# Score tiles in a third PSUM bank, and latent attention head by head, in a two-block transformer kernel

## The chip, the cores and the metric

The kernel runs on one core of a Trainium2 chip. The metric is device time in microseconds (us) from a run on the chip. Five engines work side by side, each through its own instructions in their order: TensorE (PE in the profile; its weight loads have a row of their own, PEld), VectorE (DVE), ScalarE (ACT), GpSimd (POOL) and SyncE (SP), which here only issues transfers. Matmuls write to PSUM, which has eight banks of 128 x 512 fp32 numbers; GpSimd doesn't reach PSUM.

## The reference

Everything is fp32, for 512 positions of width 1024. A first block (chunked attention, convolution, gated feed-forward) is followed by two layers with other attentions, each with a gated embedding behind it. The change touches the two later attentions:

```python
# windowed_gqa: 16 heads, 4 key heads, window of 128 around each position
logits = einsum('bqkgd,bskd->bkgqs', q_blk, k_blk) * scale - slopes * dist   # masked
probs = softmax(concatenate([logits, sink_col]))[..., :-1]
o = einsum('bkgqs,bskd->bqkgd', probs, v_blk)
return (o * silu(z)) @ w_out

# mla (latent attention): 16 heads, every position sees all 512 keys
q = (rms_norm(cq, q_norm) @ w_qb)          # 64 plain + 32 rotated columns a head
kv = (rms_norm(ckv, kv_norm) @ w_kvb)      # 64 key + 64 value columns a head
q_rope = rotate(q_rope, cos, sin)
logits = (q_nope . k_nope + q_rope . k_rope) * scale
o = softmax(logits) @ v
return (o * silu(z)) @ w_out
```

## The kernel before

Activations lie with channels on partitions, as [128, 512] tiles. A product in nearly full precision is made of three passes: each operand is split into a high and a low part (`act_hi`, `act_lo`, `w_hi`, `w_lo`), and `mm3` (L345 to L347) issues high x high, low x high and high x low into one bank. A projection tile (`tile`) is eight such triples, or two or three in latent attention, in a bank of the ring `mm`.

PSUM's eight banks are divided by `ps(tag)`: three `mm` for projections, two `s` for scores, two `pt` for turned probabilities and sums, one `o` for the attention's products.

`attention` (L598) is a generator shared by three attentions; a class `Spec` of each gives its parts. It works through pairs of heads. An item `t` is one tile of 128 queries of one head: (pair p, half hf of the queries, tile ii of the half, head hh of the pair). In order of time an item goes through

- `scores(t)`: `qk` into a bank `s` (L1406 in windowed attention, two matmuls; L1750 in latent attention, three), a row maximum on VectorE (L1419 or L1755), an exponential on ScalarE out of the bank into a tile `P`;
- `scale(t-1)`: reciprocal of the row sum (L617), and the multiplication by it, on GpSimd in both later attentions (L257);
- `turn(t-lag)`: up to four 128 x 128 transposes into a bank `pt` (L635), and a copy on ScalarE to a tile `PT`;
- `product(p, hf)` (L666): probabilities times values for both heads of the pair, each with weights of 64 columns, into the bank `o`, at raised priority. `spec.out` then multiplies by the gate (`tA` on VectorE), and splits the result into `o_hi` (ScalarE) and `o_lo` (VectorE) for the output projection.

Latent attention ran its items half by half: both heads of queries 0 to 255, their product, then both heads of queries 256 to 511 and their product. Windowed attention (`whole`) ran both halves' products together after the second.

`drive` interleaves the attention's generator with the projections (`main`) by a share, and the framework's scheduler then orders the instructions of each engine: by the order in which they were written (a raised priority goes first), by buffers that come free in their ring, and by its own reckoning of when operands are there. So the order on an engine has to be looked at in the built program.

In latent attention two pairs share a group of weights: a pair with an even number has a tile more, the rotated query columns of four heads (`evac_qr`). They go through a chain of several engines, `rotated`: copy from PSUM to `tA` (ScalarE), shuffle (VectorE, L1603), product with the sines (GpSimd, L1604), product with the cosines and sum (VectorE), `act_hi` (ScalarE), `act_lo` (VectorE), and then four transfers a pair into `Qm` (SP, L1700). Scores of the next pair need them. `put` fills the rest of `Qm` and `Km` from PSUM, with two ScalarE and two VectorE instructions each (ACT L260 `Qm<-ps_mm`, DVE L253).

Of the kernel before, what the change touches and what calls it, by code (L numbers as in the profile page):

```python
# [7 lines left out]
F32 = mybir.dt.float32  # L8
# [8 lines left out]
T = 512  # L17
# [213 lines left out]
class Kernel:  # L231
# [366 lines left out]
    def attention(self, spec, pairs, ready, s):  # L598

        nc = self.nc  # L600
        items = [(p, hf, ii, hh) for p in range(pairs) for hf in range(2) for ii in range(2) for hh in range(2)]
        n = len(items)
        P, L, PT, O = {}, {}, {}, {}

        def scores(t):
            p, hf, ii, hh = items[t]
            i = 2 * hf + ii
            ps = self.ps("s")
            spec.qk(ps, p, hh, i)
            sb = s.tile([128, spec.width], F32, tag="P", name="P", bufs=spec.lag + 1)  # L610
            st = s.tile([128, 2], F32, tag="st", name="st", bufs=8)
            P[t] = spec.softmax(ps, sb, st, p, hh, i)
            L[t] = st

        def scale(t):
            st = L.pop(t)
            nc.vector.reciprocal(out=st[:, 0:1], in_=st[:, 1:2])  # L617
            if spec.scale_act:
                self.act(P[t], P[t], AF.Copy, scale=st[:, 0:1])
            else:  # L620
                self.ts(P[t], P[t], st[:, 0:1], 1.0, MUL, MUL, eng=nc.gpsimd)

        def turn(t):
            p, hf, ii, hh = items[t]
            i = 2 * hf + ii
            js = spec.keys(i)
            if (p, hf) not in PT:
                if spec.packed:
                    PT[p, hf] = s.tile([128, 2, 5, 128], F32, tag="PT", name="PT", bufs=3)
                else:  # L630
                    PT[p, hf] = s.tile([128, 2, spec.nj, 256], F32, tag="PT", name="PT", bufs=3 if spec.whole else 2)
            ps = self.ps("pt")
            x = P.pop(t)
            for a, j in enumerate(js):
                nc.tensor.transpose(ps[:, 128 * a:128 * a + 128], x[:, 128 * a:128 * a + 128], self.ident)  # L635
            j0 = js[0] - spec.first(hf)
            if spec.packed:
                b = (2 + hf) * ii
                out = PT[p, hf][:, hh, b:b + len(js)]
            else:  # L640
                out = PT[p, hf][:, hh, j0:j0 + len(js), 128 * ii:128 * ii + 128]
            src = ps[:, :128 * len(js)].rearrange("p (a q) -> p a q", q=128)
            if spec.turn_act(t):
                self.act(out, src, AF.Copy)
            else:
                nc.vector.tensor_copy(out=out, in_=src)

        def turned(pt, hh, hf, j, c0, c1):

            a = j - spec.first(hf)  # L650
            if not spec.packed:
                return pt[:, hh, a, c0:c1]
            if c1 - c0 == 256:
                return pt[:, hh, a:a + 3:2]
            return pt[:, hh, 0 if hf else 4]

        def product(p, hf):
            if p not in O:
                O[p] = self.ps("o")
            pt = PT.pop((p, hf))  # L660
            js = spec.order(hf)

            with self.tc.high_priority():
                for n_, (j, c0, c1) in enumerate(js):
                    for hh in (1, 0):
                        nc.tensor.matmul(  # L666
                            out=O[p][64 * hh:64 * hh + 64, 256 * hf + c0:256 * hf + c1], lhsT=spec.v(p, hh, j),
                            rhs=turned(pt, hh, hf, j, c0, c1), start=(n_ == 0), stop=(n_ == len(js) - 1),
                            skip_group_check=True,
                        )  # L670
            if hf == (0 if spec.whole else 1):
                spec.out(p, O.pop(p))

        for t in range(n + spec.lag + 2):
            if t < n:
                while not ready(items[t][0]):
                    yield "wait"
                scores(t)
            if 0 <= t - 1 < n:
                scale(t - 1)  # L680
            yield
            late = t - spec.lag
            if 0 <= late < n:
                turn(late)
            if 0 <= late - 2 < n and items[late - 2][2:] == (1, 1):
                p, hf = items[late - 2][:2]
                if not spec.whole:
                    product(p, hf)
                elif hf == 1:
                    product(p, 1)  # L690
                    product(p, 0)
            yield


    def block1(self):
# [247 lines left out]
        k = self  # L943

        class Spec:
            width, nj, scale_act, lag, whole, packed = T, 4, True, 3, False, False
            keys = staticmethod(lambda i: list(range(i + 1)))
            first = staticmethod(lambda hf: 0)
            turn_act = staticmethod(lambda t: True)
# [74 lines left out]
        for c in range(4):  # L1024
            a, t = C[c], self.tmp("tA")
# [292 lines left out]
    def gqa(self, u, stat, prep, scratch):  # L1318
# [70 lines left out]
        k = self  # L1389

        class Spec:
            width, nj, scale_act, lag, whole, packed = 385, 3, False, 4, True, True
            keys = staticmethod(lambda i: list(range(max(0, i - 1), min(3, i + 1) + 1)))
            first = staticmethod(lambda hf: hf)
            turn_act = staticmethod(lambda t: True)
# [183 lines left out]
    def mla(self, u, stat):  # L1579
# [155 lines left out]
        k = self  # L1735

        class Spec:
            width, nj, scale_act, lag, whole, packed = T, 4, False, 3, False, False
            keys = staticmethod(lambda i: list(range(4)))
            first = staticmethod(lambda hf: 0)  # L1740
            turn_act = staticmethod(lambda t: True)
# [133 lines left out]
```

## Time and profile before

| | |
|---|---|
| median of 3 runs | 1380.95 us (1379.78 to 1381.73) |
| profiled execution | 1380.82 us; its span 1379.0 us |
| PE busy | 1344.8 us, 98% of the span |
| DVE, ACT, POOL busy | 65%, 49%, 18% |
| granted TensorE clock, mean | 0.992 |
| windowed attention | about 803 to 948 us of the span |
| latent attention | about 1129 to 1284 us |

Busy time of PE is counted from the start of a matmul to its modelled end, and matmuls overlap: a 128 x 512 matmul shows some 390 ns, and the next one starts 230 ns after it. So PE can be busy all the time and yet be late. What a matmul costs is read from start to start.

### The profile page before, as it was taken

Reading aid. Unit: us, or ns where it says so; the run is one execution under the profiler, and the core shown is the slowest. Engines: PE = TensorE matmul, PEld = TensorE weight load, DVE = VectorE, ACT = ScalarE, POOL = GpSimd, SP = SyncE. Lnnn points to the kernel's source line nnn. Section 1 sums busy time; section 2 is a strip of 40 time slices with the busy share of each in tenths; the row PEclk is TensorE's granted clock in tenths of the full one; section 3 lists DMA queues with packets and bytes.
Section 4 is the critical chain, followed back from the end, with each engine's and each line's share of the span. In section 5 each row is a group of like instructions: output and inputs, shape, how many; then the busy total and the mean of one; then the engine's idle time right before and its main releaser. Section 6 shows DMA issues by size and latency. Waiting matters only on the chain.

```text
span 1379.0 us, 19207 instructions
## 1 busy us (share of the span) xinstructions
PE 1344.8 (98%) x6945; PEld 1074.7 (78%) x6945; DVE 891.9 (65%) x1570; ACT 681.0 (49%) x1226; POOL 244.6 (18%) x327
## 2 busy tenths in 40 slices
PE   8999999999999999999999999999999999999996
PEld 5887777778888888888887778887887876777785
DVE  7688998875686652355534746656585766775666
ACT  5247763424564432344434455656353467776543
POOL 0000001231001110011111034433123003333212
PEclk9999999999999999999999999999999999999998
DMA  9347514557234433322224353232233220111322
GB/s 375 122 141 201 148 62 161 182 193 273 100 114 143 134 101 99 118 96 97 73 96 161 106 156 89 87 92 78 99 116 109 86 93 27 47 41 38 122 85 69
DMA packets 55744, 162.99 MB, mean 118 GB/s; under 512 B 6753, under 2 KB 9185, under 8 KB 55650
## 3 DMA queue, kind: packets, MB, share of 16 engines
q1 hardware_dynamic: 55648, 161.76, 36.0%
q8 instruction: 55, 0.90, 0.3%
q14 instruction: 39, 0.32, 0.1%
q10 hardware_dynamic: 2, 0.00, 0.0%
HBM read 140.77 MB, written 6.29 MB: 107 GB/s over the span
## 4 chain that ended last, share of the span: by engine, by line
PE 84%; DVE 8%; issue 3%; DMA 2%; ACT 2%; POOL 1%; SPq 0%; DVEq 0%; ACTq 0%; POOLq 0%
PE ps_mm L345 21%; PE ps_mm L347 21%; PE ps_mm L346 21%; PE ps_o L666 4%; PE ps_pt L635 4%; PE ps_s L1750 3%; DVE w_lo L274 2%; PE ps_s L1406 1%; DMA w_raw<-in_w_ada_dram 1%; PE ps_s L449 1%; DVE conv L253 1%; PE ps_s L959 1%; PE ps_pt L160 1%; DVE w_raw L541 1%; POOL tB L1048 1%
## 5 line engine op out<-in xcount | busy, mean ns | idle before, releaser
L345 PE MATMUL ps_mm<-act_hi,w_hi 128*128 128x512 f32 (+1 forms) x1388 | 538.5, 389 | 5.0 <-DVE ta L253 3.6
L347 PE MATMUL ps_mm<-act_hi,w_lo 128*128 128x512 f32 (+1 forms) x1388 | 533.5, 385 | 1.1 <-DVE w_lo L274 1.1
L346 PE MATMUL ps_mm<-act_lo,w_hi 128*128 128x512 f32 (+1 forms) x1388 | 533.6, 385 | 0.0
L88 ACT ACTIVATE w_hi<-w_raw 128x1024 fp32r<-128x1024 f32 (+2 forms) x202 | 202.6, 1008 | 296.9 <-PE ps_mm L346 263.5
L274 DVE TENSOR_TENSOR w_lo<-w_raw,w_hi 128x1024 fp32r<-128x1024 f32 (+2 forms) x202 | 239.8, 1190 | 149.1 <-ACT w_hi L88 145.1
L345 PEld LDWEIGHTS ps_mm<-act_hi,w_hi 128*128 128x128 f32 x1388 | 261.8, 189 | 58.5 <-ACT w_hi L88 6.1
L347 PEld LDWEIGHTS ps_mm<-act_hi,w_lo 128*128 128x128 f32 x1388 | 261.8, 189 | 54.2 <-DVE w_lo L274 2.5
L346 PEld LDWEIGHTS ps_mm<-act_lo,w_hi 128*128 128x128 f32 x1388 | 262.4, 189 | 48.9 <-issue 1.3
L257 POOL TENSOR_SCALAR P<-P,st 128x512 f32<-128x512 f32 (+2 forms) x128 | 83.3, 655 | 162.8 <-DVE st L617 157.9
L260 ACT ACTIVATE PT<-ps_pt 128x512 f32<-128x512 f32 (+3 forms) x160 | 77.6, 496 | 40.3 <-PE ps_pt L635 39.1
L253 DVE SCALAR_TENSOR_TENSOR conv<-u,vecs,conv 128x512 f32<-128x512 f32 x120 | 90.0, 751 | 1.6
L260 ACT ACTIVATE P<-P,st 128x385 f32<-128x385 f32 (+5 forms) x128 | 70.4, 557 | 35.2 <-DVE st L1419 24.4
L1206 POOL TENSOR_TENSOR val<-val,gate 128x512 f32<-128x512 f32 x22 | 28.8, 1307 | 321.5 <-ACT gate L260 321.5
L150 POOL TENSOR_TENSOR acc<-acc,sq 128x512 f32<-128x512 f32 x33 | 49.9, 1512 | 197.3 <-ACT sq L260 191.2
L635 PE MATMUL ps_pt<-ident,P 128*128 128x128 f32 x496 | 82.0, 274 | 1.3 <-POOL P L257 0.7
L635 PEld LDWEIGHTS ps_pt<-ident,P 128*128 128x128 f32 x496 | 61.6, 140 | 22.4 <-issue 2.6
L1750 PE MATMUL ps_s<-Km,Qm 128*128 128x512 f32 x192 | 60.5, 421 | 1.4 <-DMA Qm<-act_hi 0.6
L666 PE MATMUL ps_o<-PT,V 128*64 128x256 f32 (+1 forms) x544 | 60.7, 366 | 0.1
L541 DVE CUSTOM_DVE_ANT_0 w_raw<-w_raw,c,vecs 128x1024 f32<-128x1024 f32 x32 | 43.7, 1369 | 18.6 <-DMA w_raw<-in_w_ada_dram 18.4
L666 PEld LDWEIGHTS ps_o<-PT,V 128*64 128x64 f32 x544 | 35.7, 137 | 24.3 <-ACT PT L260 9.9
L1755 DVE TENSOR_REDUCE st<-ps_s 128x1 f32<-128x512 f32 x64 | 43.6, 686 | 11.9 <-PE ps_s L1750 9.5
L260 ACT ACTIVATE sq<-x 128x512 f32<-128x512 f32 (+1 forms) x62 | 33.6, 560 | 30.8 <-DVE x L250 23.7
(265 smaller groups left out, 1634.5 us busy)
## 6 DMA issues: line engine op xcount, KB each, us to landing
w_raw<-in_w_up_dram SPq DMA_DIRECT2D x44, 512.0 KB, 3.3
w_raw<-in_w_in_dram SPq DMA_DIRECT2D x32, 512.0 KB, 3.4
w_raw<-in_w_ada_dram SPq DMA_DIRECT2D x32, 512.0 KB, 3.5
w_raw<-in_a_w_in_dram SPq DMA_DIRECT2D x18, 512.0 KB, 3.4
ada<-in_w_ada_dram SPq DMA_DIRECT2D x16, 512.0 KB, 8.1
w_raw<-in_ple_w_gate_dram SPq DMA_DIRECT2D x16, 512.0 KB, 3.3
w_raw<-in_b_w_in_dram SPq DMA_DIRECT2D x14, 512.0 KB, 3.3
Q<-stage SPq DMA_DIRECT2D x48, 128.0 KB, 2.4
```

The source lines that it names most:

```text
L88: k.nc.scalar.activation(out=hi, in_=src, func=AF.Copy)
L253: return self.fix(self.nc.vector.scalar_tensor_tensor(out=out, in0=a, scalar=s, in1=b, op0=op0, op1=op1))
L257: return self.fix((eng or self.nc.vector).tensor_scalar(out=out, in0=a, scalar1=s1, scalar2=s2, op0=op0, **kw))
L260: return self.fix(self.nc.scalar.activation(out=out, in_=a, func=func, **kw))
L274: self.fix((eng or self.nc.vector).tensor_tensor(out=out, in0=x, in1=hi.bitcast(F32), op=SUB))
L345: mm(out=ps, lhsT=w[0], rhs=x[0], start=first, stop=False, **kw)
L346: mm(out=ps, lhsT=w[0], rhs=x[1], start=False, stop=False, **kw)
L347: mm(out=ps, lhsT=w[1], rhs=x[0], start=False, stop=last, **kw)
L541: self.fix(self.nc.vector.tensor_tensor_reduce(out=w, in0=w, in1=self.c, scale=0.5, scalar=self.vec("b_ada", j), op0=MUL, op1=ADD, accum_o ...
L635: nc.tensor.transpose(ps[:, 128 * a:128 * a + 128], x[:, 128 * a:128 * a + 128], self.ident)
L666: nc.tensor.matmul(out=O[p][64 * hh:64 * hh + 64, 256 * hf + c0:256 * hf + c1], lhsT=spec.v(p, hh, j), rhs=turned(pt, hh, hf, j, c0, c1), ...
L1750: nc.tensor.matmul(out=ps, lhsT=Qb[p % 2][:, qa, hh, 128 * i:128 * i + 128], rhs=Kb[p % 2][:, ka, hh], start=(a == 0), stop=(a == 2))
```

## The change

Three edits in `attention`, and a switch `headwise` in the three `Spec` classes (off in the first two attentions, on in the latent one).

- Where `whole` is set (windowed attention, and now latent attention too), every fourth item's scores (t % 4 == 3) go to a bank of the ring `mm`; the others stay in the two banks `s`.
- Latent attention's items run head by head: four query tiles of one head of the pair, then four of the other. Each (pair, half, head) has a `PT` tile of its own, five in the ring (before: two tiles with both heads). Probabilities of t % 4 in (0, 1) lie in a ring `P` of two, those of (2, 3) in the ring `sq` of two, which the sums of squares also use.
- With `whole` set, a pair's two products are issued together in latent attention, the second half's first.

```diff
-        items = [(p, hf, ii, hh) for p in range(pairs) for hf in range(2) for ii in range(2) for hh in range(2)]
+        r2 = range(2)
+        if spec.headwise:
+            items = [(p, hf, ii, hh) for p in range(pairs) for hh in r2 for hf in r2 for ii in r2]
+        else:
+            items = [(p, hf, ii, hh) for p in range(pairs) for hf in r2 for ii in r2 for hh in r2]
...
-            ps = self.ps("s")
+            ps = self.ps("mm" if spec.whole and t % 4 == 3 else "s")
             spec.qk(ps, p, hh, i)
-            sb = s.tile([128, spec.width], F32, tag="P", name="P", bufs=spec.lag + 1)
+            if spec.headwise:
+                sb = s.tile([128, T], F32, tag="P", name="P", bufs=2) if t % 4 < 2 else self.tmp("sq", 2)
+            else:
+                sb = s.tile([128, spec.width], F32, tag="P", name="P", bufs=spec.lag + 1)
...
-            if (p, hf) not in PT:
+            if spec.headwise:
+                if (p, hf, hh) not in PT:
+                    PT[p, hf, hh] = s.tile([128, 4, 256], F32, tag="PT", name="PT", bufs=5)
+            elif (p, hf) not in PT:
...
-            if spec.packed:
+            if spec.headwise:
+                out = PT[p, hf, hh][:, :, 128 * ii:128 * ii + 128]
+            elif spec.packed:
...
+            if spec.headwise:
+                return pt[hh][:, a, c0:c1]
...
-            pt = PT.pop((p, hf))
+            pt = [PT.pop((p, hf, hh)) for hh in r2] if spec.headwise else PT.pop((p, hf))
...
-            width, nj, scale_act, lag, whole, packed = T, 4, False, 3, False, False
+            width, nj, scale_act, lag, whole, packed, headwise = T, 4, False, 3, True, False, True
```

Line numbers move: 635 becomes 645, 666 becomes 680, 1406 becomes 1420, 1750 becomes 1764, 1700 becomes 1714.

TensorE in latent attention, where an even pair follows an odd one (the second of three such places, 1195 to 1203 us in the trace): before, the odd pair's first product group, and behind it the last transposes and the even pair's first scores (`Km_9005`, `Qm_9003`).

```order
L666 MATMUL ps_o<-PT,V 64x256 x8
L345 MATMUL ps_mm<-act_hi,w_hi 128x512
L346 MATMUL ps_mm<-act_lo,w_hi 128x512
L347 MATMUL ps_mm<-act_hi,w_lo 128x512
L635 MATMUL ps_pt<-ident,P 128x128 x4
L345 MATMUL ps_mm<-act_hi,w_hi 128x512
L346 MATMUL ps_mm<-act_lo,w_hi 128x512
L347 MATMUL ps_mm<-act_hi,w_lo 128x512
L635 MATMUL ps_pt<-ident,P 128x128 x8
L345 MATMUL ps_mm<-act_hi,w_hi 128x512
L1750 MATMUL ps_s<-Km_9005,Qm_9003 128x512 x2
L635 MATMUL ps_pt<-ident,P 128x128 x2
```

The same place now, from the transposes of the odd pair's fifth tile on:

```order
L645 MATMUL ps_pt<-ident,P 128x128 x4
L345 MATMUL ps_mm<-act_hi,w_hi 128x512
L346 MATMUL ps_mm<-act_lo,w_hi 128x512
L347 MATMUL ps_mm<-act_hi,w_lo 128x512
L645 MATMUL ps_pt<-ident,P 128x128 x4
L645 MATMUL ps_pt<-ident,sq 128x128 x8
L680 MATMUL ps_o<-PT,V 64x256 x16
L1764 MATMUL ps_s<-Km_9005,Qm_9003 128x512 x6
L1764 MATMUL ps_mm<-Km_9005,Qm_9003 128x512 x3
```

The group of eight ahead of the transposes is gone; twelve transposes stand in a row, a group of sixteen follows at once, and the next pair's scores come behind it. It is so at all three such places.

ScalarE at that place, before, with buffer numbers: `PT<-ps_pt` is the copy of one turned tile, `Qm0<-ps_mm` one of `put`'s two, `P<-ps_s` an exponential.

```order
L260 ACTIVATE P_10502,st_10503<-ps_s_10498,st_10503 128x512
L260 ACTIVATE act_hi_9646<-tA_10483 128x512
L260 ACTIVATE PT_10515<-ps_pt_10516 128x4x128
L260 ACTIVATE Qm0_9003<-ps_mm_10508 64x512
L260 ACTIVATE PT_10515<-ps_pt_10543 128x4x128
L260 ACTIVATE PT_10515<-ps_pt_10568 128x4x128
L260 ACTIVATE Qm0_9003<-ps_mm_10508 64x512
L260 ACTIVATE PT_10515<-ps_pt_10584 128x4x128
```

And now (`ps_pt_10550`, `ps_pt_10567` and `ps_pt_10583` are the three groups of four transposes in a row):

```order
L260 ACTIVATE PT_10522<-ps_pt_10523 128x4x128
L260 ACTIVATE act_hi_9646<-tA_10490 128x512
L260 ACTIVATE Qm0_9003<-ps_mm_10515 64x512
L260 ACTIVATE PT_10522<-ps_pt_10550 128x4x128
L260 ACTIVATE PT_10566<-ps_pt_10567 128x4x128
L260 ACTIVATE Qm0_9003<-ps_mm_10515 64x512
L260 ACTIVATE PT_10566<-ps_pt_10583 128x4x128
L260 ACTIVATE o_hi_10641<-tA_10639 128x512
```

The copies of the three turned tiles stand behind `act_hi` in both; what was after them, an exponential, is now the `o_hi` that needs the product.

TensorE in windowed attention, the scores and transposes ahead of a pair's product, before:

```order
L1406 MATMUL ps_s<-Kg,Q 128x384 x2
L635 MATMUL ps_pt<-ident,P 128x128 x2
L345 MATMUL ps_mm<-act_hi,w_hi 128x512
L1406 MATMUL ps_s<-Kg,Q 128x384 x2
L635 MATMUL ps_pt<-ident,P 128x128 x2
L1406 MATMUL ps_s<-Kg,Q 128x384 x2
L346 MATMUL ps_mm<-act_lo,w_hi 128x512
```

and now:

```order
L1420 MATMUL ps_s<-Kg,Q 128x384 x2
L645 MATMUL ps_pt<-ident,P 128x128 x2
L1420 MATMUL ps_mm<-Kg,Q 128x384 x2
L645 MATMUL ps_pt<-ident,P 128x128 x2
L1420 MATMUL ps_s<-Kg,Q 128x384 x4
L345 MATMUL ps_mm<-act_hi,w_hi 128x512
L346 MATMUL ps_mm<-act_lo,w_hi 128x512
```

One tile of scores more stands ahead of the projection's matmuls.

## Rows read from the trace of the kernel before

**Rows 1.** The page: busy time by engine, and the chain that ended last.

```profile
PE 1344.8 (98%) x6945; PEld 1074.7 (78%) x6945; DVE 891.9 (65%) x1570; ACT 681.0 (49%) x1226; POOL 244.6 (18%) x327
...
PE 84%; DVE 8%; issue 3%; DMA 2%; ACT 2%; POOL 1%; SPq 0%; DVEq 0%; ACTq 0%; POOLq 0%
PE ps_mm L345 21%; PE ps_mm L347 21%; PE ps_mm L346 21%; PE ps_o L666 4%; PE ps_pt L635 4%; PE ps_s L1750 3%; DVE w_lo L274 2%; PE ps_s L1406 1%; DMA w_raw<-in_w_ada_dram 1%; PE ps_s L449 1%; DVE conv L253 1%; PE ps_s L959 1%; PE ps_pt L160 1%; DVE w_raw L541 1%; POOL tB L1048 1%
```

**Rows 2.** Busy us by stretch: length, PE, PEld, DVE, ACT, POOL, clock, DMA.

```profile
803.00:948.00 145.00, 144.25 (x844) 115.99 (x843) 86.78 (x249) 90.18 (x230) 63.35 (x136) 1.00 0.28 84
...
1163.00:1201.00 38.00, 37.55 (x219) 26.85 (x219) 26.67 (x52) 28.63 (x63) 13.26 (x18) 1.00 0.16 42
1201.00:1239.00 38.00, 37.14 (x218) 26.65 (x218) 26.53 (x52) 29.14 (x65) 12.95 (x17) 1.00 0.16 43
```

**Rows 3.** PE in order of time: start, duration of the run, count; latent attention.

```profile
1191.39 0.40 PE L345 MATMUL ps_mm<-act_hi,w_hi 128*128 128x512 f32 x1
1191.63 0.39 PE L346 MATMUL ps_mm<-act_lo,w_hi 128*128 128x512 f32 x1
...
1203.33 0.39 PE L347 MATMUL ps_mm<-act_hi,w_lo 128*128 128x512 f32 x1
1203.64 0.65 PE L666 MATMUL ps_o<-PT,V 128*64 128x256 f32 x4
...
1203.64 1.95 PE L666 MATMUL ps_o<-PT,V 128*64 128x256 f32 x16
1205.52 1.19 PE L1750 MATMUL ps_s<-Km,Qm 128*128 128x512 f32 x4
1206.56 0.49 PE L635 MATMUL ps_pt<-ident,P 128*128 128x128 f32 x3
```

**Rows 4.** All engines in order of time, second place where an even pair follows.

```profile
1194.11 0.60 ACT L260 ACTIVATE tA<-ps_mm 128x512 f32<-128x512 f32 x1 [0.34 <-PE ps_mm L347]
...
1195.51 0.40 PE L347 MATMUL ps_mm<-act_hi,w_lo 128*128 128x512 f32 x1
...
1196.01 1.95 PE L666 MATMUL ps_o<-PT,V 128*64 128x256 f32 x16
...
1198.26 0.63 ACT L260 ACTIVATE act_hi<-tA 128x512 fp32r<-128x512 f32 x1 [1.29 <-DVE tA L250]
...
1198.92 1.07 DVE L274 TENSOR_TENSOR act_lo<-tA,act_hi 128x512 fp32r<-128x512 f32 x1 [0.63 <-ACT act_hi L260]
...
1199.84 1.03 PE L635 MATMUL ps_pt<-ident,P 128*128 128x128 f32 x8
1200.04 0.59 ACT L260 ACTIVATE Qm<-ps_mm 64x512 fp32r<-64x512 f32 x1
...
1200.53 1.06 ACT L260 ACTIVATE PT<-ps_pt 128x512 f32<-128x512 f32 x2
...
1200.66 0.68 DVE L253 SCALAR_TENSOR_TENSOR Qm<-ps_mm,Qm 64x512 fp32r<-64x512 f32 x1 [0.67 <-ACT Qm L260]
...
1201.51 0.38 PE L635 MATMUL ps_pt<-ident,P 128*128 128x128 f32 x2
...
1202.10 0.47 PE L1750 MATMUL ps_s<-Km,Qm 128*128 128x512 f32 x1 [0.21 <-DMA Qm<-act_lo]
```

**Rows 5.** PE in order of time, first such place.

```profile
1161.68 0.60 PE L635 MATMUL ps_pt<-ident,P 128*128 128x128 f32 x4
1162.50 0.41 PE L635 MATMUL ps_pt<-ident,P 128*128 128x128 f32 x2 [0.22 <-ACT PT L260]
1163.17 0.70 PE L1750 MATMUL ps_s<-Km,Qm 128*128 128x512 f32 x2 [0.26 <-DMA Qm<-act_hi]
```

**Rows 6.** Line 1750, PE and PEld: idle before it until, us, times.

```profile
  ACT P L260: 4.4, 13
```

**Rows 7.** Line 1406 and its tile's VectorE readers: ns min/median/max; idle until, us, times.

```profile
L1419 DVE CUSTOM_DVE_ANT_0 P<-ps_s,bias,nsink x64: 466/538/621, 804.9 to 943.7; 128x256 f32<-128x256 f32 x32, 128x384 f32<-128x384 f32 x32
...
  DVE st L1419: 0.5, 2
```

More of the change, by code (lines that the diff above doesn't have):

```diff
@@ L945, in block1 @@
         class Spec:
-            width, nj, scale_act, lag, whole, packed = T, 4, True, 3, False, False
+            width, nj, scale_act, lag, whole, packed, headwise = T, 4, True, 3, False, False, False
             keys = staticmethod(lambda i: list(range(i + 1)))
@@ L1391, in gqa @@
         class Spec:
-            width, nj, scale_act, lag, whole, packed = 385, 3, False, 4, True, True
+            width, nj, scale_act, lag, whole, packed, headwise = 385, 3, False, 4, True, True, False
             keys = staticmethod(lambda i: list(range(max(0, i - 1), min(3, i + 1) + 1)))
```

## The prediction

> **What bounds the kernel now.** I read the page first. PE is busy 98% of the span, and the chain that ended last runs through PE for 84% of it [rows 1]: TensorE is the engine that sets the end. So a change counts only by the time between starts of its matmuls. The stretches by engine come next [rows 2]: in windowed attention PE lacks 0.75 us of 145; in two-pair stretches of latent attention it lacks 0.45 and 0.86 of 38, at a granted clock of 1.00, while ACT works 28.6 to 29.1 of the 38 us. Busy PE hides lateness, so I went on to PE in order of time and read steps from start to start. A plain 128x512 matmul is followed 0.24 us later by the next [rows 3]; 0.23 is the usual step. Whatever exceeds such a step is either a price of the kind of matmul or a wait.
>
> **Product groups.** The change leaves the number of matmuls as it is. In latent attention it makes 8 groups of 16 matmuls from 16 groups of 8 (a matmul of the group is two records, so the trace says x16 for eight). What does a group cost beside its matmuls? Inside it, 4 records end 0.65 us after the start and 16 end after 1.95 [rows 3]: 1.30 us for 12 records, 0.217 for two, 1.73 for eight matmuls. From the group's start to the next instruction it is 1205.52 - 1203.64 = 1.88, so 0.15 more. The matmul before it takes 1203.64 - 1203.33 = 0.31 in place of 0.23, 0.08 more; the four behind it take 1206.56 - 1205.52 = 1.04 in place of 0.92, 0.12 more. A group's edges cost 0.35 us, and eight groups fewer save **2.8 us**. The order shows each group of sixteen unbroken, so I take it whole.
>
> The Trainium skill has a price for it too: "TensorEngine Tiling (Array Packing)", section Tiling Modes, says that a change of the array's division drains TensorE, and "TensorE: Matmul & The Clock Gate", section Step-by-step, puts a drain at about 128 cycles, 53 ns at 2.4 GHz. Two changes a group would make 0.11 us and eight groups 0.9 us, an estimate by the Trainium skill, and the forecast would come out 1.9 us later. The trace's 0.35 is over three times that, and it decides.
>
> **Where an even pair follows an odd one.** This place comes three times, and here the change costs. The scores of the even pair need the rotated columns, and their chain is long: `tA` starts at 1194.11 and `act_hi` at 1198.26, 4.15 us later, with ACT idle 1.29 us in front of it; what stands behind `act_hi` on ACT waits as well [rows 4]. Before, PE filled that time with a product group of the first half (1196.01, 1.9 us), and its waits were small: 1195.51 to 1196.01 is 0.50 in place of 0.31, and two transposes at 1201.51 should free PE after 0.24 but the next score starts after 0.59, so 0.5 us in all at the second place [rows 4]. At the first place the four transposes at 1161.68 take 0.82 in place of 0.44, and the two at 1162.50 take 0.67 in place of 0.24: 0.8 us [rows 5]. A smaller wait follows it, and I take 0.8 a place.
>
> Now the whole pair's product waits for the pair's last tile, since the second half is multiplied first, and nothing of the first half is left to fill with. I set it out from the start of the extra tile's last matmul, 0.43 us ahead of `tA`. PE then issues 4 transposes, 3 scores, 6 projection matmuls, 4 transposes and 3 projection matmuls: 8 transposes at 0.11 and 12 matmuls at 0.23, with 0.1 of edges and the last matmul itself 0.23, 4.0 us, and starts the twelve transposes. Two groups of four fit the two `pt` banks (to 4.9); the third needs the first one's copy. On ACT `act_hi` starts at 0.43 + 4.15 = 4.6, `Qm` follows at 5.1 and the copy at 5.6 (one behind another start 0.49 apart: 1200.04 to 1200.53), and ends at 6.2. The third group starts at 6.25, **1.35 us late**. Its own copy stands behind the second `Qm`, and that behind DVE: `act_lo` 1.07 us, then `Qm` 0.68 (5.25 to 7.05). So `Qm` 7.05, the copy 7.55 to 8.15, and the products start at 8.15 where the transposes were done at 6.8: **1.35 us late again**. That is 2.7 in place of 0.8, three times: **+5.7 us**. Behind the waiting copy on ACT stands `o_hi`, and behind that the next pair's exponentials; PE has only the group and the next scores, whose transfers are long there. Ends: if the chain ran half as long only the second wait would be left (1.35 a place, +1.7 in all); if exponentials come between as well, each adds up to 0.7 (2.1 more in all, +7.8).
>
> **Third bank for scores.** In latent attention scores waited for the exponential to free their bank for 4.4 us in 13 waits [rows 6]. Of four tiles the fourth has a bank of its own now, and the tiles beside it have one more tile's time. Nothing if the exponentials are what is late, all 4.4 if the bank is: I take half, **-2.2**, for ACT has a quarter of its time free [rows 2] but spends part of it idle in front of `act_hi` and `o_hi`. In windowed attention these waits were 0.5 us [rows 7], and PE lacks 0.75 in the whole stretch [rows 2]; the gain ends there. The price could be a projection tile that waits for its bank. A shared bank is read by one VectorE instruction of 0.54 us [rows 7]; one such wait a pair would be 8 x 0.54 = 4.3. The order shows the projection's matmuls behind the last scores and still in unbroken rows, so I take 0.
>
> **Tail, buffers.** At the end of latent attention twelve transposes stand in a row too, without `act_hi` in front: the third group waits for one copy, 0.6 us, less the 0.44 of the group between and some 0.2 of the way, **+0.4**, between 0 and 1.0. The extra `PT` tiles and the probabilities in `sq` cost nothing where the ring was read by then: the sums of squares of the latent tiles are done when the first scores start.
>
> **Sum.** -2.8 + 5.7 - 2.2 + 0.4 = +1.1 us on the profiled execution's 1380.82 us: **1381.9 us**, no change that can be told. The execution lies 0.13 us under the median of the runs, which I leave out.
>
> **Rivals.**
>
> *The place is no dearer than it was, and the banks give all.* If the third group of transposes and the products wait no longer than scores did before (+0 in place of 5.7, where the scheduler's order runs ahead of PE's arrival), and the bank waits go by 4.4: -2.8 - 4.4 + 0.4, less 0.5 in windowed attention, is -7.3; with the lower bound of 1.7 for the place it is -5.6, and I take **1375.2**. For it: the scores of the next pair no longer stand in front of missing transfers [rows 4, 5]. Against it: ACT's order puts every copy behind `act_hi`.
>
> *ScalarE becomes the pace: slower.* While the sixteen products run (3.6 us) and before them, ACT has nothing to do, some 5 us for each even pair; then four exponentials, copies, two weight splits and `put` come at once. ACT works 28.6 to 29.1 us of 38 [rows 2], so 9 are free; from there on, every further us of waiting on ACT moves PE. It decides once the idle time of a two-pair stretch goes beyond 9 us. Before, PE's edges and waits were spread; if the burst costs 1.5 us in each of three stretches and the banks give nothing back, it is -2.8 + 5.7 + 0.4 + 4.5 = +7.8, with the dearer place up to +9.9: **1388.6**. For it: those 38 us carry 16 tiles whether or not ACT stood still. Against it: copies follow each other at 0.49 us, not at their 0.6.
>
> The Trainium skill speaks for this rival: "TensorEngine Tiling (Array Packing)", section Performance Considerations (PSUM Bottleneck), says that dividing the array speeds TensorE but not the emptying of PSUM, so that the copies may become what is waited for. By that rule the time would be the rival's; the trace's quarter of free ACT time agrees only in part.
>
> *Projections wait for the third bank.* +4.3 as worked out above, on +1.1: **1386.2**. Against it: projections use their three banks in turn, and two suffice while one is emptied.
>
> **How the numbers follow.** Forecast 0.40, own range 1379 to 1385 (place 1.7 to 7.8, banks 0 to 4.4, not all at their ends). First rival 0.28, ScalarE 0.22, bank 0.10. A measurement of this kernel can tell about 0.2%, 2.8 us, from no change. Of the forecast's 0.40, 0.30 lies within that, 0.03 below and 0.07 above; the first rival gives 0.24 to faster and 0.04 to no change; ScalarE 0.20 to slower and 0.02; the bank 0.07 and 0.03. That is faster 0.27, same 0.39, slower 0.34. The range for 8 in 10 takes in the greater part of the rivals: 1374.5 to 1389.
>
> **What would show it.** The sixteen products of one group should take 3.6 us from start to the next instruction (1.88 + 1.73). At the three places PE should stand still in front of the third group of transposes, released by ACT's `PT`, and again in front of the products, 1 to 1.6 us each; no place should show scores waiting for `Qm`'s transfers. Idle time of line 1764 until ACT's exponential should fall from 4.4 to about 2. If the places show under 0.5 us each, my reading of ACT's queue is wrong and it is faster; if scores and transposes wait for ACT between the places, or projections for their bank, it is slower; a granted clock under 1.00 between 1129 and 1284 us would be something that I have not reckoned with.

## The result and the profile after

The changed kernel takes 1391.85 us (median of 6 runs, 1390.43 to 1392.88); the kernel before took 1381.34 beside it (6 runs, 1379.48 to 1383.39). The ratio is 1.0075, 95% interval 1.0063 to 1.0086: some 10.5 us slower, where 1381.9 us and no change had been forecast. The profiled execution took 1392.57 us, its span 1390.8.

The page after, busy time and chain, against [rows 1]:

```profile
PE 1345.3 (97%) x6945; PEld 1078.3 (78%) x6945; DVE 893.4 (64%) x1570; ACT 679.5 (49%) x1226; POOL 242.0 (17%) x327
...
PE 81%; DVE 10%; ACT 3%; issue 3%; DMA 2%; POOL 1%; SPq 0%; DVEq 0%; ACTq 0%; POOLq 0%
```

Work is the same to the instruction; PE's share of the chain fell from 84% to 81%, and DVE and ACT took it. So PE waits somewhere. To find the place I set the n-th matmul of one trace against the n-th of the other (both have 6945), at points between stages, where the same work lies behind both. After is 0.4 us early at 787 us (start of windowed attention), 2.9 late at 950, 2.9 still at 1131 (latent attention) and 11.8 at 1286 and at the end. So **windowed attention lost 3.3 us and latent attention 8.9**, and nothing else lost anything.

Stretches of after, by length, PE busy, granted clock, DMA, against [rows 2]:

```profile
787.00:830.00 43.00, 38.11 (x221) 0.96 0.50 139
830.00:951.00 121.00, 120.71 (x720) 1.00 0.27 78
...
1163.00:1167.00 4.00, 1.43 (x10) 0.86 0.17 43
1167.00:1174.00 7.00, 7.00 (x35) 0.59 0.20 51
1205.00:1209.00 4.00, 1.74 (x12) 1.00 0.21 52
1209.00:1213.00 4.00, 4.00 (x34) 1.00 0.34 83
1244.00:1247.50 3.50, 1.48 (x10) 1.00 0.21 53
1247.50:1254.00 6.50, 6.50 (x38) 0.74 0.22 55
```

In windowed attention everything is lost ahead of 830 us. In latent attention PE works 1.4 to 1.7 us of 3.5 or 4 at each of the three places where an even pair follows an odd one, and behind two of them its granted clock is under 1: its records lie at 0.50 (1.2 GHz in place of 2.4) for 10.2 us between 1163 and 1254, and for 3.4 us from 800.7. Before, no record between 787 and 1290 us was under 1.00. "TensorE: Matmul & The Clock Gate" of the Trainium skill, section HAM oscillation — how this bites in real kernels, tells of waits between bursts of matmuls and of a burst that then starts at the lower clock; its waits are for transfers, and longer than these. The trace agrees in the pattern, with 0.59 in the 7 us behind the first place.

The first place, all engines in order of time, against [rows 4, 5]:

```profile
1161.99 0.59 ACT L260 ACTIVATE PT<-ps_pt 128x512 f32<-128x512 f32 x1
...
1162.37 0.60 PE L645 MATMUL ps_pt<-ident,P 128*128 128x128 f32 x4
...
1162.64 1.78 POOL L257 TENSOR_SCALAR sq<-sq,st 128x512 f32<-128x512 f32 x2 [0.79 <-PE ps_mm L347]
...
1163.23 0.63 ACT L260 ACTIVATE act_hi<-tA 128x512 fp32r<-128x512 f32 x1 [0.65 <-DVE tA L250]
1163.77 0.57 ACT L260 ACTIVATE Qm<-ps_mm 64x512 fp32r<-64x512 f32 x1
...
1163.81 0.66 PE L645 MATMUL ps_pt<-ident,sq 128*128 128x128 f32 x4 [0.84 <-POOL sq L257]
...
1164.24 1.06 ACT L260 ACTIVATE PT<-ps_pt 128x512 f32<-128x512 f32 x2
...
1164.96 0.63 PE L645 MATMUL ps_pt<-ident,sq 128*128 128x128 f32 x4 [0.50 <-ACT PT L260]
...
1165.59 0.59 ACT L260 ACTIVATE Qm<-ps_mm 64x512 fp32r<-64x512 f32 x1 [0.29 <-DVE Qm L253]
...
1166.21 0.60 ACT L260 ACTIVATE PT<-ps_pt 128x512 f32<-128x512 f32 x1
...
1166.86 1.55 PE L680 MATMUL ps_o<-PT,V 128*64 128x256 f32 x6 [1.26 <-ACT PT L260]
```

PE waits three times: for GpSimd's scaling (1.0 us), for the first copy of a turned tile (0.66), and for the last copy, which stands behind `act_hi` and both `Qm` (products at 1166.86, 1.33 late). These are steps from the last transpose's start to the next instruction's, less what the step takes without a wait: 0.11 to another transpose, 0.2 to a product group. The first wait I had not forecast; the sum, 3.0 us here and 2.8 at the other two, I had put at 2.7.

The second place, PE alone. Here the clock held, and the group shows its price, against [rows 3]:

```profile
1206.65 0.63 PE L645 MATMUL ps_pt<-ident,sq 128*128 128x128 f32 x4 [0.50 <-ACT PT L260]
1208.55 3.67 PE L680 MATMUL ps_o<-PT,V 128*64 128x256 f32 x32 [1.26 <-ACT PT L260]
1212.15 1.19 PE L1764 MATMUL ps_s<-Km,Qm 128*128 128x512 f32 x4
```

1212.15 - 1208.55 is 3.60 for sixteen products. At the first place the same group takes 1166.86 to 1173.34, 6.48 us.

Scores of latent attention, idle until, us, times, against [rows 6]:

```profile
  ACT P L260: 1.2, 6
  ACT Qm L260: 0.9, 2
  ACT sq L260: 0.2, 1
```

The waits for exponentials did fall, from 4.4 to 1.4.

Start of windowed attention, the transfers of Q and PE, against [rows 7]:

```profile
795.49 0.28 PE L436 MATMUL ps_pt<-w_hi,act_lo 128*128 128x256 f32 x1
795.62 3.16 SPq L1321 DMA_DIRECT2D Q<-stage  x4
...
800.61 0.71 PE L1420 MATMUL ps_s<-Kg,Q 128*128 128x256 f32 x2 [4.84 <-DMA Q<-stage]
```

The first scores stand in PE's order before Q is there, and PE waits 5.1 us from start to start. Before, 28 projection matmuls (the 24 of one tile and the first four of the next) stood ahead of the first scores, which came at 804.40; now they come behind the scores.

### The profile page after: what moved, and what is told of

It reads as the page before. It is cut to its first block, busy times and chain, and to the rows that moved or that the text cites. A ratio compares the mean times of both kernels' runs of the same rounds, so it can differ in the third digit from the quotient of the medians.

```text
span 1390.8 us, 19189 instructions
## 1 busy us (share of the span) xinstructions
PE 1345.3 (97%) x6945; PEld 1078.3 (78%) x6945; DVE 893.4 (64%) x1570; ACT 679.5 (49%) x1226; POOL 242.0 (17%) x327
## 4 chain that ended last, share of the span: by engine, by line
PE 81%; DVE 10%; ACT 3%; issue 3%; DMA 2%; POOL 1%; SPq 0%; DVEq 0%; ACTq 0%; POOLq 0%
PE ps_mm L345 21%; PE ps_mm L346 20%; PE ps_mm L347 20%; PE ps_o L680 4%; PE ps_pt L645 3%; DVE w_lo L274 2%; PE ps_s L1764 2%; PE ps_s L1420 1%; DMA w_raw<-in_w_ada_dram 1%; DVE conv L253 1%; DVE act_lo L274 1%; PE ps_s L449 1%; PE ps_s L973 1%; DVE tA L250 1%; PE ps_pt L160 1%
## 5 line engine op out<-in xcount | busy, mean ns | idle before, releaser
L257 POOL TENSOR_SCALAR P<-P,st 128x256 f32<-128x256 f32 (+2 forms) x96 | 60.1, 632 | 134.0 <-DVE st L624 131.4
L680 PE MATMUL ps_o<-PT,V 128*64 128x256 f32 (+1 forms) x544 | 63.5, 385 | 3.8 <-ACT PT L260 3.8
L645 PE MATMUL ps_pt<-ident,P 128*128 128x128 f32 x368 | 62.2, 276 | 0.9 <-POOL P L257 0.5
L680 PEld LDWEIGHTS ps_o<-PT,V 128*64 128x64 f32 x544 | 38.5, 144 | 28.9 <-ACT PT L260 10.9
L645 PEld LDWEIGHTS ps_pt<-ident,P 128*128 128x128 f32 x368 | 44.5, 140 | 17.5 <-POOL P L257 3.1
L1764 PE MATMUL ps_s<-Km,Qm 128*128 128x512 f32 x144 | 45.2, 418 | 0.8 <-DVE Qm L253 0.4
L260 ACT ACTIVATE gate<-gate 128x512 f32<-128x512 f32 x22 | 13.9, 633 | 64.2 <-DVE gate L253 58.5
```

The lines of the kernel that those rows point to most:

```text
L257: return self.fix((eng or self.nc.vector).tensor_scalar(out=out, in0=a, scalar1=s1, scalar2=s2, op0=op0, **kw))
L260: return self.fix(self.nc.scalar.activation(out=out, in_=a, func=func, **kw))
L680: nc.tensor.matmul(out=O[p][64 * hh:64 * hh + 64, 256 * hf + c0:256 * hf + c1], lhsT=spec.v(p, hh, j), rhs=turned(pt, hh, hf, j, c0, c1), ...
L1764: nc.tensor.matmul(out=ps, lhsT=Qb[p % 2][:, qa, hh, 128 * i:128 * i + 128], rhs=Kb[p % 2][:, ka, hh], start=(a == 0), stop=(a == 2))
```

## The experiments

Time ahead of 787 us, where all kernels are alike, varied between the profiled executions by 3.8 us, because stretches at half clock at 30, 243 and 312 us come and go. So beside the timed ratio each kernel is judged by two stretches of its own profile: how many us later than in before the n-th matmul comes, gained between the points that are 787 and 950 us in before (windowed attention) and 1131 and 1286 (latent attention), and for how long the clock was granted at half in each. Both are of one execution of each kernel. Where a stage is as before and shows no half clock, its shift is 0.0 to -0.2 us; smaller differences aren't told apart here.

| kernel | ratio to before (95%) | windowed, us | at half | latent, us | at half |
|---|---|---|---|---|---|
| changed | 1.0075 (1.0063-1.0086) | +3.3 | 3.4 | +8.9 | 10.2 |
| e1 windowed part alone | 1.0030 (1.0019-1.0042) | +3.5 | 6.8 | -0.2 | 0 |
| e2 latent part alone | 1.0061 (1.0049-1.0073) | +1.4 | 3.4 | +7.9 | 6.8 |
| e3 first half first | 1.0049 (1.0035-1.0063) | +3.3 | 6.8 | +3.6 | 0 |
| e4 wait filled | 1.0056 (1.0044-1.0068) | +3.4 | 6.8 | +4.6 | 0 |
| e5 heads, no third bank | 0.9994 (0.9985-1.0002) | 0.0 | 0 | -0.3 | 0 |
| e6 third bank, no heads | 1.0000 (0.9991-1.0009) | 0.0 | 0 | +0.5 | 0 |
| e7 windowed from pair 2 | 0.9994 (0.9985-1.0004) | -0.6 | 0 | -0.2 | 0 |
| e8 = e6 and e7 | 0.9993 (0.9985-1.0002) | -0.7 | 0 | +0.6 | 0 |
| e9 fourth tile only | 1.0051 (1.0035-1.0067) | 0.0 | 0 | +6.7 | 6.8 |
| e10 eighth tile only | 0.9982 (0.9972-0.9992) | +1.4 | 3.4 | -1.5 | 0 |
| e11 = e5 and e7 | 0.9983 (0.9972-0.9994) | -0.6 | 0 | -0.3 | 0 |
| e12 = e10 and e7 | 0.9976 (0.9966-0.9985) | -0.6 | 0 | -1.3 | 0 |

My first theory: the whole pair's product leaves nothing to fill the places, the waits there cost their length and then the clock; windowed attention loses by the order at its start. Rivals: ScalarE is the pace, and windowed attention's loss is chance.

**e1, windowed part alone.** Latent attention's `Spec` as before:

```diff
-width, nj, scale_act, lag, whole, packed, headwise = T, 4, False, 3, True, False, True
+width, nj, scale_act, lag, whole, packed, headwise = T, 4, False, 3, False, False, False
```

> The third bank in windowed attention alone; latent attention as before. Theory: the first scores of windowed attention now stand in TensorE's order ahead of the projection tile that used to cover the transfer of Q, so TensorE waits some 5 us there and is granted half its clock behind it (3.9 us lost at the start), and the rest of windowed attention gives 0.7 back: 3.2 us over the kernel before, about 1384.5, with the half clock at 800 us in the trace. Rival (windowed attention costs nothing, the half clock there was chance): 1381.3, no half clock at 800 us.

Measured 1385.9 us; before was 1381.64 there. Windowed attention +3.5, with half clock from 802.0: it is no chance.

**e2, latent part alone.**

```diff
-ps = self.ps("mm" if spec.whole and t % 4 == 3 else "s")
+ps = self.ps("mm" if spec.headwise and t % 4 == 3 else "s")
```

> Latent attention as changed (head by head, one group, third bank); windowed attention as before. Theory: the changed kernel's 10.5 us less the 3.2 of windowed attention: 7 to 8.5 us over the kernel before, 1388.5 to 1390, with half clock again behind the first and third place where an even pair follows an odd one. Rival (windowed attention costs nothing): 1391.8.

Measured 1390.52, slightly over the range, because unchanged windowed attention had 3.4 us at half clock in the profile too (+1.4). e10 shows the same; before, e5, e6 and e9, with windowed attention unchanged too, don't: behind its small waits half clock comes in some executions. In latent attention it came at the second and third place, where the first and third had been expected from the changed kernel.

**e3, first half's product ahead.**

```diff
-            if hf == (0 if spec.whole else 1):
+            if hf == (0 if spec.whole and not spec.headwise else 1):
                 spec.out(p, O.pop(p))
...
-                    product(p, 1)
-                    product(p, 0)
+                    product(p, 0 if spec.headwise else 1)
+                    product(p, 1 if spec.headwise else 0)
```

> The changed kernel, but in latent attention the first half's product is written ahead of the second's, so that it stands on TensorE between the last two groups of transposes, where TensorE waited. Theory (the waits of 1.3 us before the products and 0.66 before the last transposes cost their length and the clock behind them): waits 3 x 2.0 us and 5 us of half clock go, some 2.8 us of group edges come back as the groups are 16 again: 8 us under the changed kernel, about 1384. Rival (ScalarE is the pace, so that the waits only move to the next scores): within 2 us of the changed kernel, 1390 to 1392.

Measured 1388.77: 3 us better than the changed kernel, where 8 were expected. Half clock is gone from latent attention, but at each place PE still waits 0.82 to 0.86 for the scaling and 0.48 ahead of the group, and the groups are 16 again.

**e4, the wait filled.** Nothing gets shorter; PE only has something to do while it waits for the last copy:

```diff
+                if spec.headwise and hf == 1 and p in (1, 3, 5):
+                    for m in range(6):
+                        nc.tensor.matmul(out=O[p][:, 0:128], lhsT=self.ident, rhs=pt[1][:, m % 4, 0:128],
+                                         start=True, stop=True, skip_group_check=True)
```

> The changed kernel with six matmuls of 128 columns that compute nothing of use (their bank is overwritten) in front of the products of pairs 1, 3 and 5: they need the copy before the last one, and so run in the 1.34 us that TensorE waits there. No wait becomes shorter. Theory (the wait takes TensorE's granted clock down): no half clock behind the places, the products take 3.6 us in all three, 5 us under the changed kernel, about 1387. Rival (the clock falls for the products themselves, or for the two waits ahead of them): half clock at 1166 and 1248 us as before, time 1391 to 1392.

Measured 1389.02. PE at the second place:

```profile
1203.37 0.63 PE L645 MATMUL ps_pt<-ident,sq 128*128 128x128 f32 x4 [0.50 <-ACT PT L260]
1203.83 1.53 PE L680 MATMUL ps_o<-PT,ident 128*128 128x128 f32 x12
1205.29 3.67 PE L684 MATMUL ps_o<-PT,V 128*64 128x256 f32 x32
1208.90 1.66 PE L1768 MATMUL ps_s<-Km,Qm 128*128 128x512 f32 x6
```

The products come 1.92 us behind the third group of transposes, as in the changed kernel (1208.55 - 1206.65 = 1.90), and take 3.61. No half clock is left in latent attention, which loses 4.6 instead of 8.9: **in these two profiles 4.3 us of the 8.9 were the clock**, and work without use bought them back. At half clock the groups of the first and third place took 6.48 and 5.29 us in place of 3.60, which is 4.6 together. The timed runs give less: e4 came out 2.8 us under the changed kernel where 5 had been expected, and 7.4 over the kernel before where the changed one was 10.5 over. The executions that were not profiled may hold half clock in other places.

**e5, heads without the third bank** (windowed attention as before). From here on each `Spec` has a rule `bank(t)`:

```diff
-ps = self.ps("mm" if spec.whole and t % 4 == 3 else "s")
+ps = self.ps("mm" if spec.bank(t) else "s")
+bank = staticmethod(lambda t: False)        # e5, both later attentions
```

> Latent attention head by head and in one group as changed, but every score tile in the two banks of before; windowed attention as before. Theory: the third bank is worth 2 to 4 us in latent attention (scores waited 4.4 us for the exponential in the kernel before, 0.1 in the changed one), so latent attention is lost by 10 to 12 us in place of the 8 of the run with the third bank; time about 1391 to 1393. Rival (the third bank gives nothing, since the wait only moves to the next copy): latent attention +7 to +8, about 1389.

Measured 1382.03 beside 1382.31: **both theories fell.** (The first theory's 0.1 us of waiting in the changed kernel is a wrong figure; it is 1.4, as shown above.) With heads in turn and the pair's products in one group, latent attention isn't slower at all. PE at its second place:

```profile
1198.68 0.60 PE L645 MATMUL ps_pt<-ident,P 128*128 128x128 f32 x4
1199.94 0.65 PE L645 MATMUL ps_pt<-ident,sq 128*128 128x128 f32 x4 [0.66 <-POOL sq L257]
1200.35 0.48 PE L345 MATMUL ps_mm<-act_hi,w_hi 128*128 128x512 f32 x1
...
1201.14 0.60 PE L645 MATMUL ps_pt<-ident,sq 128*128 128x128 f32 x4
1201.49 0.48 PE L345 MATMUL ps_mm<-act_hi,w_hi 128*128 128x512 f32 x1
...
1202.27 0.40 PE L345 MATMUL ps_mm<-act_hi,w_hi 128*128 128x512 f32 x1
1202.99 3.67 PE L680 MATMUL ps_o<-PT,V 128*64 128x256 f32 x32 [0.32 <-ACT PT L260]
```

The same copies are waited for, but three and four projection matmuls, 1.6 us, stand between. Six of the seven are the key tile of the next pair (its copy `Km<-ps_mm` starts at 1203.56), the last one begins the tile behind it. Waits remain: PE stands idle for 0.66 and 0.32 us here, 0.65 and 0.33 at the third place, and once for 1.30 at the first, before the scaling. So the third bank takes the filler away. How? New theory: banks of one ring are given out in the order in which they are asked for. A score tile in the projections' ring asks ahead of the projection tiles written behind it; as long as its own operands are on their way, they can't start either.

**e6, the third bank alone in latent attention**, `bank(t)` is `t % 4 == 3` there, items half by half, two products a pair.

> The kernel before with one thing changed: every fourth score tile of latent attention goes to the third projection bank. Items half by half, 16 groups of products, windowed attention as before. Theory: the waits of 4.4 us for the exponential mostly go and nothing else comes: latent attention 2 to 4 us shorter, no half clock between 1129 and 1284 us, about 1378.5. Rival (a score tile in the projections' ring holds up the next projection as it did at the start of windowed attention): latent attention longer by 1 to 4 us, about 1384.

Measured 1382.28 beside 1382.31: neither. Waits of the scores for the exponential fall to 0.9 us, and in their place come waits for `Qm`, from 1.0 to 2.7 us, and of the transposes for the scaling, from 3.2 to 5.4. What the scores (line 1767) wait for now, PE and PEld:

```profile
  ACT Qm L260: 2.7, 5
  ACT P L260: 0.9, 4
  DVE Qm L253: 0.4, 1
```

**e7, windowed attention from the second pair on**, `bank(t)` is `t >= 8 and t % 4 == 3` there; latent attention as before.

> The third bank in windowed attention only from the second pair on; latent attention as before. Theory (the loss of 3.3 us came from the two tiles of the first pair, which take places in the ring of projection banks ahead of the next projection tile and so hold it back): the projection tile stands before the first score again, no wait of 5 us at 800 us and no half clock through it; windowed attention 0.5 to 0.9 us shorter than before, about 1380.9. Rival (the loss is one of the third bank as such): about 1384.5.

Measured 1381.86 beside 1382.31, which by itself is no difference; but windowed attention is 0.6 us shorter than before, where e1 had it 3.5 longer. The two tiles of the first pair made all of the loss. PE at the start of windowed attention, a projection tile in the gap again:

```profile
796.02 0.28 PE L436 MATMUL ps_pt<-w_hi,act_lo 128*128 128x256 f32 x1
796.14 0.40 PE L345 MATMUL ps_mm<-act_hi,w_hi 128*128 128x512 f32 x1
...
804.57 0.40 PE L1422 MATMUL ps_s<-Kg,Q 128*128 128x256 f32 x2
```

**e8, e6 and e7 together.**

> The third bank in both attentions, in windowed attention from the second pair on, with latent attention half by half and 16 groups as before. Theory: the gains of the last two kernels add up: 2.5 to 5 us under the kernel before, 1376.5 to 1379. Rival (third bank holds up projections in latent attention): 1383 to 1385.

Measured 1381.31 beside 1382.31, not distinguishable: neither the theory nor the rival came, and the theory of e6 fell here too.

**e9 and e10, one tile of eight** in the third bank of latent attention, heads in turn, one group; windowed attention as before. Of a pair's eight, `t % 8 == 3` is the fourth and `t % 8 == 7` the eighth:

```diff
-bank = staticmethod(lambda t: False)
+bank = staticmethod(lambda t: t % 8 == 3)   # e9; e10: t % 8 == 7
```

> Latent attention head by head and in one group, but only the fourth of a pair's eight score tiles in the third projection bank (the eighth back in the scores' banks); windowed attention as before. Theory (banks of one ring are given out in the order in which they are asked for; the fourth tile of an even pair asks ahead of the next pair's key tile and can't start until that pair's queries are there, so the key tile's matmuls, which fill TensorE's wait at the place in the run without the third bank, are held back): the three places are bare again, 2.8 us of waits each and half clock behind one or two of them, latent attention 5 to 8 us longer than before, about 1388. Rival (it is the number of score tiles in flight, whichever): half of the run with both tiles, some +4, and the same as the run with the eighth tile alone.

> As the run with the fourth tile alone, but it is the eighth tile of each pair that goes to the third bank. Theory: the eighth tile's scores come when its pair's queries have long been there, and nothing that fills the places asks for a bank behind it; the order keeps three and four matmuls of the key tile between the transposes and the products, the waits there stay under 1 us a place, no half clock; latent attention between 2 us shorter and 1 longer than before, about 1381.5. Rival (tiles in flight): +4, about 1386.

Measured 1389.44 and 1380.38 beside 1382.28. The same number of tiles in the third bank, and 9 us apart. TensorE's order at the first place, e9 and then e10:

```
L645 MATMUL ps_pt<-ident,P 128x128 x4
L645 MATMUL ps_pt<-ident,sq 128x128 x8
L680 MATMUL ps_o<-PT,V 64x256 x16
L1767 MATMUL ps_s<-Km_9005,Qm_9003 128x512 x6
L1767 MATMUL ps_mm<-Km_9005,Qm_9003 128x512 x3
L345 MATMUL ps_mm<-act_hi,w_hi 128x512
```

```
L645 MATMUL ps_pt<-ident,sq 128x128 x4
L345 MATMUL ps_mm<-act_hi,w_hi 128x512
L346 MATMUL ps_mm<-act_lo,w_hi 128x512
L645 MATMUL ps_pt<-ident,sq 128x128 x2
L1767 MATMUL ps_s<-Km_9005,Qm_9003 128x512 x6
L645 MATMUL ps_pt<-ident,sq 128x128 x2
L347 MATMUL ps_mm<-act_hi,w_lo 128x512
L345 MATMUL ps_mm<-act_hi,w_hi 128x512
L346 MATMUL ps_mm<-act_lo,w_hi 128x512
L347 MATMUL ps_mm<-act_hi,w_lo 128x512
L680 MATMUL ps_o<-PT,V 64x256 x16
```

In e9 the key tile's first matmul comes right behind the fourth tile's scores (`ps_mm<-Km`), and these need the very `Qm` that is being made. In e10 nothing holds the key tile. PE at the second place of e9:

```profile
1203.29 0.65 PE L645 MATMUL ps_pt<-ident,sq 128*128 128x128 f32 x4 [0.66 <-POOL sq L257]
1204.44 0.63 PE L645 MATMUL ps_pt<-ident,sq 128*128 128x128 f32 x4 [0.50 <-ACT PT L260]
1206.33 3.67 PE L680 MATMUL ps_o<-PT,V 128*64 128x256 f32 x32 [1.26 <-ACT PT L260]
1209.93 1.66 PE L1767 MATMUL ps_s<-Km,Qm 128*128 128x512 f32 x6
```

and of e10:

```profile
1199.06 0.60 PE L645 MATMUL ps_pt<-ident,sq 128*128 128x128 f32 x4
1199.42 0.48 PE L345 MATMUL ps_mm<-act_hi,w_hi 128*128 128x512 f32 x1
...
1200.20 0.39 PE L345 MATMUL ps_mm<-act_hi,w_hi 128*128 128x512 f32 x1
1200.92 3.67 PE L680 MATMUL ps_o<-PT,V 128*64 128x256 f32 x32 [0.33 <-ACT PT L260]
```

The new theory had forecast 1388 and 1381.5, the rival (tiles in flight) 1386 for both. These runs bear out the first and not the second.

**e11, e5 and e7 together.**

> Latent attention head by head and in one group without the third bank, windowed attention with it from the second pair on: the two parts that each came out at or just under the kernel before. Theory: they add up, 0.3 and 0.7 us under the kernel before, about 1381; no half clock between 787 and 1290 us. Rival: any of the half-clock stretches comes back with another order, 1384 or more.

Measured 1380.5 beside 1382.28, ratio 0.9983 (0.9972 to 0.9994): as the theory had it, if a little more, and no half clock came in either attention.

**e12, e10 and e7 together.**

> The eighth tile of each latent pair in the third bank, one group a pair, and windowed attention with the third bank from the second pair on. Theory: 0.7 us from windowed attention, 0 to 2 from latent attention: 1379.5 to 1381.5, the best that this change has to give. Rival (eighth tile harmful as the fourth): 1385 or more.

Measured 1379.5 (12 runs, 1377.41 to 1381.36) beside 1382.28: ratio 0.9976 (0.9966 to 0.9985), **faster than both kernels**. The gain is 0.24%. In its profile no record of either attention is at half clock. Against e11 the timed runs can't tell it.

## Why the prediction was wrong

**The step that failed is "Third bank for scores".** It put the gain at -2.2 and the price at 0: "The order shows the projection's matmuls behind the last scores and still in unbroken rows, so I take 0". I reckoned with a projection that waits for the release of a bank. The price lies in the order itself: that the matmuls stood *behind* the scores was the cost. The fourth tile of a latent pair costs 7.0 us (e9 against e5, +6.7 and -0.3), the first pair's two tiles in windowed attention 3.9 (+3.3 against -0.6 in e7). Only the eighth tile gains, 1.2, and only alone (e10 against e5); beside the fourth it doesn't (e2 has both and as much half clock as e9, and loses 1.2 us more).

In the terms of the sum: it gave +1.1, and the two stages show 3.3 + 8.9 = 12.2. Of the 11.1 between, 3.3 are windowed attention, which stood at 0; some 4.3 are the clock, which had no term; 2.2 are the gain of the third bank, which didn't come. The rest, 1.3, isn't told apart.

- *Windowed attention at 0.* I read 803 to 948 us [rows 2, 7]. The loss lies at 795 to 804, ahead of that stretch, and I had not compared the order there. Behind it the change gains 0.6 (e7), what "the gain ends there" with -0.5 to -0.75 had said.
- *The waits for exponentials* fell as forecast, from 4.4 to 1.4 us, but in latent attention the time didn't follow: e6 moved it by +0.5. The next operand (`Qm`, scaled probabilities) was as late. And the 4.4 were too large to start from: [rows 6] is idle time of PE and PEld together. For PE alone, the kernel before shows at line 1750:

```profile
  ACT P L260: 0.3, 1
```

  The other 4.1 us are gaps on the row of the weight loads, which run beside matmuls; a gap there need not cost as much on PE. How much of it did is not shown.
- *Product groups, -2.8.* Sixteen products take 3.60 us from start to start where the clock is full; 3.61 had been forecast. The saving itself wasn't tried alone; e5, which has it, gains 0.3 in all. But PE stands still 4.5 of the 160 us from 1130 there, and 2.6 in the kernel before (length, PE busy, clock, DMA; before, then e5), so some 2 of the 2.8 us can be there, an estimate from these two rows:

```profile
1130.00:1290.00 160.00, 157.41 (x906) 1.00 0.16 46
1130.00:1290.00 160.00, 155.51 (x907) 1.00 0.16 46
```

- *Even-pair places, +5.7.* Length nearly right (2.8 to 3.0 each for 2.7), in part by luck: the wait ahead of the third group was 0.66 where I had 1.35, and the wait for the scaling, which I hadn't, made up for it. The cause was wrong: I blamed the first half's product, which had filled the place. e5 has no such product there, and stands idle for 0.66 and 0.32 at its second place. The next key tile fills it, if the ring lets it.
- *What no step held: the clock.* I took a wait at its length, and named a clock under 1.00 there only as something not reckoned with. At bare places TensorE fell to 1.2 GHz: in the three kernels with all three waits at each place and nothing in them (changed, e2, e9) 6.8 to 10.2 us of latent attention ran at half, in the other eleven, before among them, none. e4's profile prices it at 4.3 us, its timed runs at about 3.
- *Tail, +0.4.* A wait of 0.9 us for an exponential came there instead of one for a copy. It goes with the eighth tile in the third bank: PE idles there for 0.91 us in the changed kernel, e4, e10 and e12, for 0.42 in e9 and 0.21 in e5 and e11, which lack it.

Of the rivals, the first (1375.2) did not come: its places were as dear as forecast, and the banks gave nothing. "ScalarE becomes the pace" named a time close by (1388.6), but its mechanism isn't seen: scores wait 1.4 us in all for exponentials, and filling one wait took back half of the stage's loss in the profiles. "Projections wait for the third bank" had the right place and a wrong mechanism: not a wait for a release, but the order in which the ring is given out.

"Perfetto Trace Analysis" of the Trainium skill, section Optimizing Tensor Performance, advises that independent matmul groups rotate through different PSUM banks, so that emptying one overlaps with the next. The measurements agree only in part, and they decide. Here it depends on whose rotation a group joins: one more bank for scores, taken from the projections' ring, made latent attention 7.0 us longer in e9 and 1.2 shorter in e10, both against e5.

Two things stay open. That the ring gives banks in the order asked is argued: the two orders, e7, and e9 against e10 fit it; the rule itself wasn't taken out. And that the filled wait kept the clock up in e4 rests on three places of one execution, while three of the nine bare places kept it too.

## What to carry to other kernels

Before a tile moves to another ring of buffers, ask who asks for a buffer behind it, and whether that work was the filler of some wait: a tile with late operands in a ring holds up every tile behind it, without any wait for a release in the trace. Compare the built order ahead of the stage too, not only in it. And price a wait of TensorE at more than its length, where it can take the clock with it; a little work in the gap, useful or not, gave 4.3 us back in e4's profile.

## What the hardware showed that I had not expected

- Three waits close together (1.0, 0.66 and 1.33 us, with four short transposes between them) were followed by a granted clock of 0.50 in place of 1.00, from within the last wait or up to 0.5 us behind it. So it was at six of the nine such places in three profiles (changed, e2, e9), and not at the other three. With the last of the three waits filled (e4's profile), at none of three.
- At half clock two records of the product group take 0.43 us (1169.04 to 1169.47) in place of 0.217, so the group of sixteen took 6.48 us in place of 3.60.
- The clock can fall for less: windowed attention of before, unchanged, showed 3.4 us at half from 805.0 in e2 and 804.1 in e10, behind waits of 1.1 and 0.7 us, and was 1.4 us longer there. Four other profiles of it show none.
